# Rotary embedding on one core: all slab loads in SyncE's ring, the tables in ScalarE's ring as 4 KB descriptors

## The chip, the cores and the metric

The kernel runs on one core of a Trainium2 chip. The metric is device time in microseconds (us), lower is better. Three runs of the kernel before gave 163.01, 164.19 and 165.96 us; the median is 164.19. One more execution was profiled.

## The reference

The input `x` is 16 x 512 x 1024 in float32, 33.55 MB; the output has the same size. Each row of 1024 is 16 heads of 64. `cos` and `sin` have one row of 32 numbers for each of the 512 positions (64 KB each), and all batches and heads share them.

```
x = x.reshape(batch, seq, num_heads, head_dim)
x1, x2 = x[..., :half_dim], x[..., half_dim:]
cos = cos[None, :, None, :]
sin = sin[None, :, None, :]
rotated = np.concatenate([
    x1 * cos - x2 * sin,
    x1 * sin + x2 * cos
], axis=-1)
```

## The kernel before, in words

**Tiling.** The batch is cut into 8 slabs (s = 0 to 7) of two batch entries, 4 MB each. A slab is one SBUF tile of 128 partitions x 8192 float32: partition p holds 8 consecutive rows (32 KB, contiguous in DRAM). Six tiles exist (`slots = 6`), so slab 6 reuses the tile of slab 0, and slab 7 that of slab 1, once the earlier slab's store has landed.

**Loads.** `load(s)` (L59 to L63) issues one 4 MB DMA. Slabs 0 to 5 go on SyncE's queue (SP), slabs 6 and 7 on GpSimd's (POOL). On SP the order is: slab 0, `cos`, `sin` (L72), slabs 1 to 5. The loads of slabs 6 and 7 are issued from the end of the main loop (L141), after the stores of slabs 0 and 1.

**Tables.** `cos` and `sin` land as 64 partitions x 256 float32 (8 positions in a partition, 1 KB each, 64 descriptors a table). GpSimd casts them to bf16 (L91). Since partitions p and p + 64 of a slab need the same positions, four matmuls (L96) with selection matrices of 0 and 1 (or -1) `pick` (built by GpSimd, L81 to L87) copy the 64 rows to 128 partitions and lay out `cos|cos` and `sin|-sin` for the 64 columns of a head in PSUM tile `acc`. VectorE copies that to the bf16 tile `tab` (L102). Every multiplication in the main loop reads `tab`.

**Main loop.** Slabs 1 to 5 are one pass each, slabs 0, 6 and 7 two passes of half a slab. A pass is: ScalarE casts float32 to bf16 (L121, into the upper part of the tile's own bytes); VectorE multiplies twice by the tables (L131) and adds with the halves of each head swapped (L134); ScalarE casts back to float32 (L137). After the last pass of a slab ScalarE's queue issues the 4 MB store (L139). A cast in (L121) of a whole slab takes 7.0 us, a cast out (L137) 7.0 us, of half a slab 3.6 us each; VectorE needs 13.3 us for a slab.

**Order of the queues.** The program's framework orders the instructions of each engine. In the trace ScalarE's order is, from slab 2 on: cast in of slab s + 2, store of slab s, cast out of slab s + 1, and so on. So the store of slab s stands behind a cast that waits for the load of slab s + 2. At the end: cast in 6a, store 4, cast out 5, cast in 6b, store 5, cast out 6a, cast in 7a, cast out 6b, cast in 7b, store 6, cast out 7a, cast out 7b, store 7 (a and b are half slabs).

DMA packets of a slab are 32 KB, 8 for each of the core's 16 DMA engines. The profile calls SP's ring q1, ScalarE's ring q10 and GpSimd's q0. The framework has 8 completion counters for the DMAs that SP and ScalarE issue, and takes them in turn. A DMA waits until the earlier user of its counter has landed: the sixth slab load (slab 5) is issued at 13.18 us, when slab 0 has landed.

Of the kernel before, what the change touches and what calls it, by code (L numbers as in the profile page):

```python
# [2 lines left out]

# [4 lines left out]


@with_exitstack  # L10
def kernel(
    ctx: ExitStack,
    tc: tile.TileContext,
    x: bass.AP,
    cos: bass.AP,
    sin: bass.AP,
    num_heads: int,
    out: bass.AP,
):
    nc = tc.nc  # L20
    P = nc.NUM_PARTITIONS

    batch, seq, dim = x.shape
    nh = num_heads
    hd = dim // nh
    half = hd // 2
    bf16 = mybir.dt.bfloat16
    f32 = mybir.dt.float32

    nb = 2  # L30
    slots = 6
    nslabs = batch // nb
    rpp = nb * seq // P
    W = rpp * dim
    SP = seq // rpp
    TW = rpp * half

    out_flat = out.rearrange("b s h d -> b s (h d)")

    singles = ctx.enter_context(tc.tile_pool(name="singles", bufs=1))  # L40
    slabs = ctx.enter_context(tc.tile_pool(name="slabs", bufs=slots))
    psum = ctx.enter_context(tc.tile_pool(
        name="psum", bufs=1, space=bass.MemoryType.PSUM))


    def dram(t, s, a=0, n=W):
        return bass.AP(tensor=t.tensor, offset=t.offset + s * nb * seq * dim + a,
                       ap=[[W, P], [1, n]])


    def view(t, offset, *dims):
        return dataclasses.replace(t, offset=t.offset + offset,
                                   ap=[t.ap[0], *[list(d) for d in dims]])


    slab = {}


    def load(s):  # L59

        queue = nc.sync if s < slots else nc.gpsimd
        slab[s] = slabs.tile([P, W], f32, tag="slab", name="slab")
        queue.dma_start(out=slab[s], in_=dram(x, s))  # L63


    load(0)


    cos_sb = singles.tile([SP, TW], f32, tag="cos_sb")
    sin_sb = singles.tile([SP, TW], f32, tag="sin_sb")  # L70
    for t, src in ((cos_sb, cos), (sin_sb, sin)):
        nc.sync.dma_start(out=t, in_=bass.AP(  # L72
            tensor=src.tensor, offset=src.offset, ap=[[TW, SP], [1, TW]]))

    for s in range(1, slots):
        load(s)

    pick = singles.tile([SP, 2 * P], bf16, tag="pick")  # L80
    nc.gpsimd.memset(pick, 0.0)  # L81
    for g in range(2):
        part = view(pick, g * P, (SP, P // SP), (1, SP))
        nc.gpsimd.affine_select(  # L84
            out=part, in_=part, compare_op=mybir.AluOpType.not_equal,
            fill=1.0 - 2.0 * g, base=0, pattern=[[0, P // SP], [-1, SP]],
            channel_multiplier=1)  # L87

    tab1 = singles.tile([SP, 2 * TW], bf16, tag="tab1")
    for i, t in enumerate((cos_sb, sin_sb)):  # L90
        nc.gpsimd.tensor_copy(out=view(tab1, i * TW, (1, TW)), in_=t)  # L91

    acc = psum.tile([P, 2 * rpp * hd], f32, tag="acc")
    for i in range(2):
        for h in range(2):
            nc.tensor.matmul(  # L96
                view(acc, i * rpp * hd + h * half, (hd, rpp), (1, half)),
                view(pick, i * h * P, (1, P)),
                view(tab1, i * TW, (half, rpp), (1, half)),
                start=True, stop=True)  # L100
    tab = singles.tile([P, 2 * rpp * hd], bf16, tag="tab")
    nc.vector.tensor_copy(out=tab, in_=acc)  # L102

    passes = []
    for s in range(nslabs):
        n = rpp if 1 <= s < nslabs - 2 else rpp // 2
        passes += [(s, r, n) for r in range(0, rpp, n)]  # L110


    def halves(u):
        s, r, n = u
        t = slab[s].bitcast(bf16)
        return [view(t, (2 * r + i * n) * dim, (1, n * dim)) for i in range(2)]


    def cast(u):
        s, r, n = u  # L120
        nc.scalar.copy(out=halves(u)[0], in_=view(slab[s], r * dim, (1, n * dim)))  # L121


    cast(passes[0])
    for i, u in enumerate(passes):
        s, r, n = u
        if i + 1 < len(passes):
            cast(passes[i + 1])
        lo, up = halves(u)
        for t, a in ((up, 0), (lo, rpp * hd)):  # L130
            nc.vector.tensor_mul(  # L131
                out=t, in0=lo,
                in1=view(tab, a + r * hd, (hd, n), (0, nh), (1, hd)))
        nc.vector.tensor_add(  # L134
            out=up, in0=up, in1=view(lo, half, (hd, n * nh), (-half, 2), (1, half)))

        nc.scalar.copy(out=view(slab[s], r * dim, (1, n * dim)), in_=up)  # L137
        if r + n == rpp:
            nc.scalar.dma_start(out=dram(out_flat, s), in_=slab[s])  # L139
            if s + slots < nslabs:  # L140
                load(s + slots)  # L141


# [1 line left out]
_INS = ['x', 'cos', 'sin', 'num_heads']  # L145
_OUTS = [((16, 512, 16, 64), 'float32')]

_NUMBERS = {'num_heads': 16}


# [26 lines left out]
```

## Time and profile before

The profiled execution took 163.56 us, 0.63 us under the median of the three runs. Its span, from the first to the last instruction that the profile shows, is 161.8 us, so 1.8 us lie around the span. Times below are us from the span's start.

| slab | load issued | load landed | store issued | store landed |
|---|---|---|---|---|
| 0 | 0.74 | 13.16 | 37.48 | 61.13 |
| 1 | 2.37 | 23.39 | 51.31 | 87.83 |
| 2 | 3.00 | 33.10 | 65.16 | 108.41 |
| 3 | 3.49 | 45.46 | 93.97 | 120.59 |
| 4 | 4.02 | 64.82 | 107.93 | 130.26 |
| 5 | 13.18 | 93.94 | 121.45 | 139.96 |
| 6 | 61.77 | 95.16 | 135.62 | 149.62 |
| 7 | 88.40 | 114.53 | 149.80 | 160.90 |

`cos` and `sin` were issued at 1.17 and 1.74 and had landed at 13.52 and 13.86. "Landed" is the last of the 16 completion records of a DMA, one from each DMA engine. A store "issued" at 37.48 is the moment at which ScalarE's queue hands it to the DMA rings. Read a row from left to right for one slab's way through the kernel, and the columns "landed" together for what the DMA engines did: 16 slabs of 4 MB went through them.

| engine | busy, us | share of the span |
|---|---|---|
| DVE (VectorE) | 108.5 | 67% |
| ACT (ScalarE) | 113.2 | 70% |
| POOL (GpSimd) | 3.0 | 2% |
| PE (TensorE) | 1.0 | 1% |

### The profile page before, as it was taken

The page shows a single profiled execution, that of the slowest core. Times are in us where ns is not written, and L with a number is a line of the kernel's source. Part 1 is how long each engine was busy: PE and PEld are TensorE (multiplying, and loading weights), DVE is VectorE, ACT ScalarE, POOL GpSimd, SP SyncE. Part 2 cuts the span into 40 slices and gives each one's busy share as a digit, 9 for nine tenths or more (in the row PEclk, how much of TensorE's full clock was granted, in tenths as well). Part 3 has the DMA queues.
Part 4 walks back from the last instruction along what each step waited for, and adds up shares of the span by engine and source line. Part 5 has one row for each costly group of instructions (what it writes and reads, how often), then busy time and mean ns, then how long its engine had stood idle before and what let it go on. Part 6 is the DMA issues. An engine that isn't in the chain of part 4 may idle for free.

```text
span 161.8 us, 157 instructions
## 1 busy us (share of the span) xinstructions
PE 1.0 (1%) x4; PEld 0.5 (0%) x4; DVE 108.5 (67%) x34; ACT 113.2 (70%) x23; POOL 3.0 (2%) x11
## 2 busy tenths in 40 slices
PE   0002000000000000000000000000000000000000
PEld 0000000000000000000000000000000000000000
DVE  0002899999899989989991000999991999991000
ACT  3007929999999999999500079995799999928000
POOL 2001000000000001000001000000000000000000
DMA  7999999999999999999899999999999999996996
GB/s 243 405 389 421 462 446 389 454 454 389 405 470 421 405 470 421 413 454 429 389 478 429 389 486 421 397 478 421 405 470 421 421 462 413 429 454 284 389 389 259
DMA packets 2464, 67.24 MB, mean 416 GB/s; under 512 B 288, under 2 KB 416, under 8 KB 416
## 3 DMA queue, kind: packets, MB, share of 16 engines
q10 hardware_dynamic: 1152, 33.55, 48.1%
q1 hardware_dynamic: 1024, 25.30, 37.1%
q0 software_dynamic: 288, 8.39, 12.1%
HBM read 33.69 MB, written 33.55 MB: 416 GB/s over the span
## 4 chain that ended last, share of the span: by engine, by line
ACT 34%; issue 23%; DMA 13%; DVE 12%; another core or an unknown queue 9%; SPq 1%; ACTq 0%
ACT slab L137 23%; DMA slab<-in_x_dram 13%; ACT slab L121 11%; DVE slab L131 8%; DVE slab L134 4%; SPq L72 1%; SPq L63 0%; ACTq L137 0%; ACTq L121 0%
## 5 line engine op out<-in xcount | busy, mean ns | idle before, releaser
L131 DVE TENSOR_TENSOR slab<-slab,tab 128x4096 bf16<-128x4096 bf16 (+1 forms) x22 | 71.7, 3261 | 22.2 <-ACT slab L121 21.7
L121 ACT CAST slab<-slab 128x4096 bf16<-128x4096 f32 (+1 forms) x11 | 56.6, 5153 | 29.3 <-DMA slab<-in_x_dram 29.3
L137 ACT CAST slab<-slab 128x4096 f32<-128x4096 bf16 (+1 forms) x11 | 56.6, 5154 | 6.6 <-DVE slab L134 6.5
L134 DVE TENSOR_TENSOR slab<-slab 128x4096 bf16<-128x4096 bf16 (+1 forms) x11 | 35.9, 3261 | 0.3
L102 DVE CAST tab<-acc 128x1024 bf16<-128x1024 f32 x1 | 1.2, 1224 | 15.1 <-PE acc L96 15.1
L63 POOL DMA_DIRECT2D slab<-in_x_dram x2 | 1.2, 611 | 73.4 <-DMA out_dram<-slab 73.4
L121 ACT ACT_TABLE_LOAD x1 | 1.3, 1283 | 0.7 <-PEq L158 0.7
L96 PE MATMUL acc<-tab,pick 64*128 64x256 bf16 x4 | 1.0, 403 | 14.0 <-POOL tab L91 14.0
L91 POOL CAST tab<-cos_sb 64x256 bf16<-64x256 f32 x1 | 0.4, 389 | 11.9 <-DMA cos_sb<-in_cos_dram 11.9
L84 POOL TENSOR_SCALAR_AFFINE_SELECT pick<-pick 64x128 bf16<-64x128 bf16 x2 | 0.5, 286 | 0.1
L96 PEld LDWEIGHTS <-pick 64*128 64x128 bf16 x4 | 0.5, 121 | 14.1 <-issue 12.5
L91 POOL CAST tab<-sin_sb 64x256 bf16<-64x256 f32 x1 | 0.4, 393 | 0.0
L81 POOL MEMSET pick<- 64x256 bf16 x1 | 0.3, 304 | 0.3 <-POOLq L158 0.3
L158 POOL MEMSET const-float32-0.0<- 128x1 f32 x1 | 0.1, 103 | 0.2 <-issue 0.2
L158 POOL MEMSET const-bfloat16-1.0<- 128x1 bf16 x1 | 0.1, 106 | 0.0
L158 POOL MEMSET const-uint8-127<- 128x1 uint8 x1 | 0.1, 106 | 0.0
L158 POOL MEMSET const-float32-1.0<- 128x1 f32 x1 | 0.1, 103 | 0.0
## 6 DMA issues: line engine op xcount, KB each, us to landing
out_dram<-slab ACTq DMA_DIRECT2D x8, 4096.0 KB, 23.0
slab<-in_x_dram SPq DMA_DIRECT2D x6, 4096.0 KB, 36.0
slab<-in_x_dram POOLq DMA_DIRECT2D x2, 4096.0 KB, 29.8
cos_sb<-in_cos_dram SPq DMA_DIRECT2D x1, 64.0 KB, 12.3
sin_sb<-in_sin_dram SPq DMA_DIRECT2D x1, 64.0 KB, 12.1
```

Of the source, the lines that this page charges most:

```text
L63: queue.dma_start(out=slab[s], in_=dram(x, s))
L72: nc.sync.dma_start(out=t, in_=bass.AP(tensor=src.tensor, offset=src.offset, ap=[[TW, SP], [1, TW]]))
L81: nc.gpsimd.memset(pick, 0.0)
L84: nc.gpsimd.affine_select(out=part, in_=part, compare_op=mybir.AluOpType.not_equal, fill=1.0 - 2.0 * g, base=0, pattern=[[0, P // SP], [-1 ...
L91: nc.gpsimd.tensor_copy(out=view(tab1, i * TW, (1, TW)), in_=t)
L96: nc.tensor.matmul(view(acc, i * rpp * hd + h * half, (hd, rpp), (1, half)), view(pick, i * h * P, (1, P)), view(tab1, i * TW, (half, rpp) ...
L102: nc.vector.tensor_copy(out=tab, in_=acc)
L121: nc.scalar.copy(out=halves(u)[0], in_=view(slab[s], r * dim, (1, n * dim)))
L131: nc.vector.tensor_mul(out=t, in0=lo, in1=view(tab, a + r * hd, (hd, n), (0, nh), (1, hd)))
L134: nc.vector.tensor_add(out=up, in0=up, in1=view(lo, half, (hd, n * nh), (-half, 2), (1, half)))
L137: nc.scalar.copy(out=view(slab[s], r * dim, (1, n * dim)), in_=up)
L158: nc = _bacc.Bacc("TRN2", target_bir_lowering=False, num_devices=1)
```

## The change

All eight slab loads are issued on SP's queue; the loads of slabs 6 and 7 still come from the same place in the loop and wait for the stores of slabs 0 and 1. The two tables leave SP's queue for ScalarE's, where they are issued at the start. Each table is now 16 descriptors of 4 KB: 32 positions to a partition, on every eighth partition of a tile `raw` of 128 x 1024 float32 (`cos` on partitions 0, 8, 16, ..., `sin` on 4, 12, 20, ...). VectorE clears `raw` first. GpSimd casts all of `raw` to bf16 in one instruction, and builds 12 selection matrices in place of 2 (one memset of 128 x 1536 and 12 selects). Each of the four parts of `acc` is now the sum of four matmuls, one for each group of 8 positions in a partition, so 16 matmuls in place of 4. `tab` holds the same numbers in the same places, and the main loop is unchanged.

```diff
     def load(s):
-
-        queue = nc.sync if s < slots else nc.gpsimd
         slab[s] = slabs.tile([P, W], f32, tag="slab", name="slab")
-        queue.dma_start(out=slab[s], in_=dram(x, s))
+        nc.sync.dma_start(out=slab[s], in_=dram(x, s))
...
+    TR = 16
+    TQ = seq // TR // rpp
+    TC = seq * half // TR
+    raw = singles.tile([P, TC], f32, tag="raw")
+    nc.vector.memset(raw, 0.0)
+    def load_tables(queue):
+        for i, src in enumerate((cos, sin)):
+            to = dataclasses.replace(
+                raw, offset=raw.offset + 4 * i * raw.ap[0][0],
+                ap=[[P // TR * raw.ap[0][0], TR], [1, TC]])
+            queue.dma_start(out=to, in_=bass.AP(
+                tensor=src.tensor, offset=src.offset, ap=[[TC, TR], [1, TC]]))
     load(0)
-    cos_sb = singles.tile([SP, TW], f32, tag="cos_sb")
-    sin_sb = singles.tile([SP, TW], f32, tag="sin_sb")
-    for t, src in ((cos_sb, cos), (sin_sb, sin)):
-        nc.sync.dma_start(out=t, in_=bass.AP(
-            tensor=src.tensor, offset=src.offset, ap=[[TW, SP], [1, TW]]))
+    load_tables(nc.scalar)
     for s in range(1, slots):
         load(s)
-    pick = singles.tile([SP, 2 * P], bf16, tag="pick")
+    pick = singles.tile([P, 3 * TQ * P], bf16, tag="pick")
     nc.gpsimd.memset(pick, 0.0)
-    for g in range(2):
-        part = view(pick, g * P, (SP, P // SP), (1, SP))
-        nc.gpsimd.affine_select(
-            out=part, in_=part, compare_op=mybir.AluOpType.not_equal,
-            fill=1.0 - 2.0 * g, base=0, pattern=[[0, P // SP], [-1, SP]],
-            channel_multiplier=1)
+    for g in range(3):
+        for j in range(TQ):
+            part = view(pick, (g * TQ + j) * P + j, (SP, P // SP), (TQ, TR))
+            nc.gpsimd.affine_select(
+                out=part, in_=part, compare_op=mybir.AluOpType.not_equal,
+                fill=-1.0 if g == 2 else 1.0, base=-4 if g else 0,
+                pattern=[[0, P // SP], [-(P // TR), TR]], channel_multiplier=1)
-    tab1 = singles.tile([SP, 2 * TW], bf16, tag="tab1")
-    for i, t in enumerate((cos_sb, sin_sb)):
-        nc.gpsimd.tensor_copy(out=view(tab1, i * TW, (1, TW)), in_=t)
+    raw_b = singles.tile([P, TC], bf16, tag="raw_b")
+    nc.gpsimd.tensor_copy(out=raw_b, in_=raw)
     acc = psum.tile([P, 2 * rpp * hd], f32, tag="acc")
-    for i in range(2):
-        for h in range(2):
+    for g, at in ((0, 0), (0, half), (1, rpp * hd), (2, rpp * hd + half)):
+        for j in range(TQ):
             nc.tensor.matmul(
-                view(acc, i * rpp * hd + h * half, (hd, rpp), (1, half)),
-                view(pick, i * h * P, (1, P)),
-                view(tab1, i * TW, (half, rpp), (1, half)),
-                start=True, stop=True)
+                view(acc, at, (hd, rpp), (1, half)),
+                view(pick, (g * TQ + j) * P, (1, P)),
+                view(raw_b, j * TW, (half, rpp), (1, half)),
+                start=j == 0, stop=j == TQ - 1)
```

## The prediction

> **What bounds the kernel now.** I read the page from the top: busy shares, slices, queues. No compute engine passes 70%, but the DMA row is at 9 in all but a few slices, and the queues add up.
>
> ```profile
> span 161.8 us, 157 instructions
> ...
> DMA  7999999999999999999899999999999999996996
> ...
> q10 hardware_dynamic: 1152, 33.55, 48.1%
> q1 hardware_dynamic: 1024, 25.30, 37.1%
> q0 software_dynamic: 288, 8.39, 12.1%
> ```
>
> The three shares make 97.3%, 157.4 of 161.8 us: the 16 DMA engines work nearly all the time. By windows they moved 429 GB/s with one ring (13.2 to 37.5 us), 424 with two (41.5 to 61.5) and 437 with three (66 to 90): how the work is spread over rings hardly changes the rate. What can be gained are the three places where they stand still: slice 0 (start), the 6 in slice 36, the 6 in the last. I open the end with the DMA view for 140 to 161.8 us (40 slices of 0.55 us).
>
> ```profile
> DMA  9999590959699890000909109090909169090000
> GB/s 481 481 421 541 240 721 0 721 240 661 301 421 541 361 601 0 0 0 0 962 0 902 60 0 962 0 962 0 962 0 902 60 301 661 0 962 0 0 0 0
> ```
>
> Slices 15 to 18 (148.2 to 150.4 us) move nothing. Single empty slices mean nothing (packets are counted where they start, and last 1.2 us); four in a row are a hole. Why it is there, the timeline says:
>
> ```profile
> 146.16 3.60 ACT L137 CAST slab<-slab 128x4096 f32<-128x4096 bf16 x1 [3.56 <-DVE slab L134]
> 149.80 0.34 ACTq L139 DMA_DIRECT2D out_dram<-slab  x1
> ```
>
> Store 7 is issued at 149.80, after the last cast out, while store 6 had landed at 149.62: the rings were empty. Back to back, stores land 9.68 us apart (130.26, 139.96, 149.62). Store 7 lands 11.28 after store 6, so the hole costs 1.60 us. Then I asked why ScalarE was late with its last cast. The waits show it:
>
> ```profile
> ACT slab L121 <- DMA slab<-in_x_dram: 29.3, 3, 15.0
> ...
> DVE tab L102 <- PE acc L96: 15.1, 1, 15.1
> PE acc L96 <- POOL tab L91: 14.0, 1, 14.0
> ...
> POOL tab L91 <- DMA cos_sb<-in_cos_dram: 11.9, 1, 11.9
> ```
>
> The lower three are the table chain at the start, over by 16.3 us. The 15.0 us is the cast of slab 5, from 78.97 to 93.97: slab 5 lands at 93.94. Its load was in SP's ring long before; it crept, because from 66 us on three rings share the engines, as the DMA view for 68 to 84 us shows:
>
> ```profile
> q0 software_dynamic: 72, 2.36, 34.7%
> q1 hardware_dynamic: 70, 2.29, 33.3%
> q10 hardware_dynamic: 70, 2.29, 33.2%
> ```
>
> A third each. Slab 6 (q0), needed later, took a third of the bandwidth from slab 5 (q1), needed next, and landed 1.2 us after it.
>
> **The change part by part.**
>
> *Slabs 6 and 7 behind slab 5 on SP.* Nothing changes up to 61.1 us (store 0 lands, slab 6 is issued). From then on there are two rings; rows for two rings are at hand: store 0 and load 4 ran side by side from 41.8 to 61.13, so a slab takes 19.4 us of a half share. Store 1: 61.1 + 19.4 = 80.5 (now 87.8). Slab 5, after slab 4 at 64.8: 84.2 (now 93.9). Slab 6: 103.6 (now 95.2). Slab 7, whose load is issued when store 1 lands at 80.5 and so waits in the ring: 123.0 (now 114.5). Stores 2 and 3: 99.9 and 119.3. Issue costs 0.33 to 0.58 us of SP's time a load, and behind them SP has only the end's waits; on POOL nothing stood behind them either. So these cost 0; the cover is the load before it in the ring, and if that ran dry, a new start costs 1.4 us (store 7: 11.1 from issue to landing, less 9.7).
>
> *ScalarE with these landings,* in the order it has now, 7.0 and 3.6 us a cast: cast 5 and store 3 at 84.2; cast out 4 91.2 to 98.2; cast 6a waits for slab 6 at 103.6, with it store 4; cast out 5 to 114.2, cast 6b, store 5 at 114.3; cast out 6a to 121.3; cast 7a waits for slab 7, 123.0 to 126.6; cast out 6b 130.2, cast 7b, store 6 at 130.3. From the start of cast 7a to the end of the last cast out it is now 128.33 to 149.76, 21.4 us: store 7 at 123.0 + 21.4 = 144.4. Every store is issued before the one ahead of it has landed (store 4 103.6 before 119.3, store 5 114.3 before about 130, store 6 130.3 before 140, store 7 144.4 before 149.6). The 29.3 us of waits move, they don't vanish, but the hole closes. After 13 slabs' worth (130.26 now) three stores remain: 130.26 + 3 x 9.68 = 159.30 against 160.90. Gain 1.6; bounds 0 (hole comes back whole) and 1.6 (there is no more in it).
>
> *Tables in DMA time.* Slab 0 to slab 1 is 10.23 us between landings, slab 1 to slab 2 9.71: the tables cost 0.52 now. Later, 128 KB at the 434 GB/s of whole slabs (4.19 MB in 9.7 us) are 0.3. Bounds 0.3 and 0.52 (no better than now): I take a gain of 0.2, the slab rate being nearest to 4 KB pieces on 16 engines, though the bytes are few.
>
> [...]
>
> *Tables in time for VectorE.* `tab` is ready at 16.28 now and first read at 16.82, when ScalarE's first cast ends. After: the memset of `raw`, 128x1024, bounded by the copy L102 of that size, 1.22 us, from 0.74 to 2.0; two issues on ScalarE's queue at 0.34 to 0.58, to 3.2 (ScalarE is idle until slab 0 is there, so nothing queues behind them but the 1.28 us table load). Start in a ring beside a full one: store 0 was issued at 37.48 and had first packets at 41 to 41.8, so up to 4.3; to an empty one 1.4. Two rounds of packets of 1.2 us: landed between 6 and 10. GpSimd: memset of 6 times the elements of the 0.30 one, 1.8; 12 selects at 0.29, 3.4: done at 6.0, before the tables at the late end. Cast of 4 times the elements of 0.39: 1.6. 16 matmuls at 0.25 (four took 1.01): 4.0, at most 0.41 each, 6.6. Copy 1.2. So `tab` at 13 to 17, at worst 19.4. First use is at 16.8, and 0.2 later with slab 0's landing. A delay up to 3.4 us is still hidden: the second half slab's add ends at 30.4 and ScalarE, busy with slab 1, takes it at 33.84. Beyond that it would eat into ScalarE's idle time before cast 5. So 0, and at the worst 0.
>
> **Sum.** 163.56 - 1.6 - 0.2 = 161.8 against the profiled execution. The median of the three runs is 0.63 higher; one execution and three runs cannot say which is typical, so I add half of it: **162.1 us**, 1.3% under 164.19.
>
> **The rivals.**
>
> *A: the hole stays.* The gap closes only if slab 7 lands by 126.8: store 7 must be issued 1.4 us before 149.6, and needs 21.4 from the landing. My 123.0 leaves 3.8. For it: cast 7a waits for slab 7 now, which it did not before (landed 114.5, cast at 128.3), so slab 7's lateness goes into the end. Against it: half shares were steady from 44 to 61 us. With a landing at 128.3, store 7 is at 149.8 again: 163.4 to 164.2, no change.
>
> *B, slower: a load held up by a completion counter.* The waits of SP's queue have a load that waited for another load, though its tile was free:
>
> ```profile
> SPq L63 <- DMA slab<-in_x_dram: 8.7, 1, 8.7
> ```
>
> The counters are taken in turn by 8, and the change puts 18 DMAs on them in place of 16. Eight places back is a DMA that landed long ago in every order I can think of; but if slab 7's load had to wait for store 3 (119.3) instead of store 1, the ring would be dry from 103.6. It would start at 120.7 beside store 4, land 19.4 later near 140, and store 7 would go at 161.5 and land 11.1 later, at 172.6: 175 us. It decides where slab 7 lands after 128.3, and makes over 2% from 131.6 (3.3 us more). The same holds if the engines' new order puts a cast that waits for slab 7 ahead of older casts out.
>
> *C: faster than the hole.* Nothing to gain is left but the start (1.9 us idle until the first packet) and the end; 160.9 or less needs the runs to fall low, as 163.01 did under 164.19.
>
> *D: the change does nothing:* the tables are off the path already (0.54 us of slack at 16.82), and the bytes are the same. If slab 5's early landing is no use because the end is decided elsewhere, this is A.
>
> **How the numbers follow.** Forecast 0.64, A 0.20, B 0.12, C 0.04. The likeliest one's own range is 160.8 to 163.4: 162.1 less the 1.2 us that the lowest run lay under the median, and up to the sum with no gain from the tables and the whole 0.63, and 0.7 of run-to-run difference. The range reaches through A, whose runs may lie as high as its 164.2 and 0.9 more: 160.8 to 165.1; beyond lies B. The bounds are 160.9 and 167.5, 2% either way, about what a measurement of this kernel can tell from no change. Faster: C and the low edge of the forecast, 0.11. Slower: B and little else, 0.13. Same: 0.76.
>
> **What would show it.** Right: no q0 at all; slab 5 cast near 84, slab 6 near 104, slab 7 near 123; no run of empty slices near 149; store 7 issued before store 6 lands, its issue to landing well over 11.1 us; ScalarE's 15.0 us wait broken into some 5 us each before slabs 5 and 6; L102 ending before 17.5. Wrong: a cast of slab 7 after 127, a wait of SP for anything but store 0, store 1 and slab 0, or ScalarE's order changed. A `tab` after 20 us would mean that the tables starve beside a full ring.

## The result and the profile after

The changed kernel takes 162.09 us (median of 6 runs, 161.88 to 162.21), the kernel before 163.81 in the same comparison (163.01 to 166.01). The ratio is 0.9912, with a 95% interval of 0.9883 to 0.994: a gain of 0.9%, small but outside the noise. The profiled execution took 161.88 us, its span is 160.1. Some executions of the kernel before, e1, e8 and e9 are 2 to 13 us longer, and those over 1.5% above the kernel's fastest are left out of the ratios; in the two that were profiled (e1 and e9) two of the 16 DMA engines finish slabs up to 15 us after the others, the reason is not known, and none of the 44 runs with the tables in ScalarE's ring was left out.

The page of the changed kernel, the same lines as before:

```profile
span 160.1 us, 200 instructions
...
DMA  7999999999999999999999999999999999999994
...
q1 hardware_dynamic: 1152, 33.55, 49.3%
q10 hardware_dynamic: 1216, 33.69, 48.8%
```

q0 is gone, and so is the 6 in slice 36: from slice 1 to 38 every digit is 9. The shares make 98.1% of 160.1, 157.1 us, the work of before (157.4); what went is idle time. Where three rings had a third of the engines each, the DMA view of 68 to 84 us now shows two halves:

```profile
q1 hardware_dynamic: 121, 3.44, 49.8%
q10 hardware_dynamic: 119, 3.38, 48.9%
```

The DMA view of 138.4 to 160.1 us, the last 21.7:

```profile
DMA  0909092992909092962909091948909090920000
GB/s 0 967 0 966 0 846 121 483 483 121 846 0 966 0 846 121 664 302 121 846 0 966 0 906 60 785 181 362 604 0 966 0 966 0 846 121 0 0 0 0
```

Up to the last packets there are never two empty slices in a row; in the kernel before there were four (148.2 to 150.4 us). The timeline of ScalarE shows the middle of it, from slab 5 on (start, duration, instruction, and in brackets the idle time ahead of it):

```profile
84.17 7.02 ACT L129 CAST slab<-slab 128x8192 bf16<-128x8192 f32 x1 [3.85 <-DMA slab<-in_x_dram]
...
103.53 3.60 ACT L129 CAST slab<-slab 128x4096 bf16<-128x4096 f32 x1 [5.42 <-DMA slab<-in_x_dram]
...
122.95 3.60 ACT L129 CAST slab<-slab 128x4096 bf16<-128x4096 f32 x1 [1.88 <-DMA slab<-in_x_dram]
...
140.63 3.60 ACT L145 CAST slab<-slab 128x4096 f32<-128x4096 bf16 x1 [3.46 <-DVE slab L142]
144.27 0.34 ACTq L147 DMA_DIRECT2D out_dram<-slab  x1
```

The one wait of 15.0 us has become three, for slabs 5, 6 and 7: 3.85, 5.42 and 1.88 us, 11.2 in all. The landings and stores against the forecast:

| | before | forecast | after |
|---|---|---|---|
| slab 5 landed | 93.94 | 84.2 | 84.15 |
| slab 6 landed | 95.16 | 103.6 | 103.51 |
| slab 7 landed | 114.53 | 123.0 | 122.87 |
| store 1 landed | 87.83 | 80.5 | 80.42 |
| last store issued | 149.80 | 144.4 | 144.27 |
| store 6 landed | 149.62 | 149.6 | 149.44 |
| last store landed | 160.90 | 159.3 | 159.09 |
| `tab` ready | 16.28 | 13 to 17, at worst 19.4 | 18.70 |

The last store is handed over 5.2 us before store 6 has landed, and lands 9.65 us after it, back to back, not 11.28.

### The profile page after: what moved, and what is told of

It reads as the page before. It is cut to its first block, busy times and chain, and to the rows that moved or that the text cites. A ratio compares the mean times of both kernels' runs of the same rounds, so it can differ in the third digit from the quotient of the medians.

```text
span 160.1 us, 200 instructions
## 1 busy us (share of the span) xinstructions
PE 3.6 (2%) x16; PEld 2.3 (1%) x16; DVE 109.3 (68%) x35; ACT 113.3 (71%) x23; POOL 4.7 (3%) x18
## 4 chain that ended last, share of the span: by engine, by line
DMA 50%; DVE 21%; ACT 8%; issue 7%; PE 2%; POOLq 1%; ACTq 0%; DVEq 0%; SPq 0%
DMA slab<-in_x_dram 26%; DMA out_dram<-slab 17%; DVE slab L139 14%; DMA raw<-in_sin_dram 6%; DVE slab L142 6%; ACT slab L145 5%; ACT slab L129 3%; PE acc L104 2%; DVE tab L110 1%; POOLq L180 1%; DVE raw L69 1%; ACTq L77 0%; POOLq L99 0%; DVEq L139 0%; SPq L61 0%
## 5 line engine op out<-in xcount | busy, mean ns | idle before, releaser
L129 ACT CAST slab<-slab 128x4096 bf16<-128x4096 f32 (+1 forms) x11 | 56.6, 5153 | 23.1 <-DMA slab<-in_x_dram 23.1
L104 PE MATMUL acc<-raw_b,pick 128*128 128x256 bf16 x16 | 3.6, 415 | 13.9 <-POOL raw_b L99 13.9
L104 PEld LDWEIGHTS <-pick 128*128 128x128 bf16 x16 | 2.3, 142 | 14.7 <-issue 11.3
L93 POOL TENSOR_SCALAR_AFFINE_SELECT pick<-pick 128x32 bf16<-128x32 bf16 x12 | 2.1, 257 | 0.1
L69 DVE MEMSET raw<- 128x1024 f32 x1 | 0.9, 912 | 1.0 <-PEq L166 1.0
L89 POOL MEMSET pick<- 128x1536 bf16 x1 | 1.4, 1377 | 0.3 <-POOLq L166 0.3
L99 POOL CAST raw_b<-raw 128x1024 bf16<-128x1024 f32 x1 | 1.0, 1036 | 8.5 <-DMA raw<-in_sin_dram 8.5
```

Of the source, the lines that this page charges most:

```text
L69: nc.vector.memset(raw, 0.0)
L93: nc.gpsimd.affine_select(out=part, in_=part, compare_op=mybir.AluOpType.not_equal, fill=-1.0 if g == 2 else 1.0, base=-4 if g else 0, pat ...
L99: nc.gpsimd.tensor_copy(out=raw_b, in_=raw)
L104: nc.tensor.matmul(view(acc, at, (hd, rpp), (1, half)), view(pick, (g * TQ + j) * P, (1, P)), view(raw_b, j * TW, (half, rpp), (1, half)), ...
```

## The experiments

**Theory and rivals.** Theory O (order): the gain is the hole ahead of the last store. It closes because slab 5 no longer shares the engines with slab 6 from a third ring, and it needs nothing of the tables' new path. Rival T: the tables make the gain. Rival R: it is GpSimd's ring that is slow. A second pair is about the end: *threshold* (slab 7 may be late until 126.8 at no cost, and from there each us costs one) against *every-us* (its lateness always shows) and *bytes alone* (it never does).

**e1_loads_only**: one line of the kernel before.

```diff
-        queue = nc.sync if s < slots else nc.gpsimd
+        queue = nc.sync
```

> The kernel before, with one edit: all eight slab loads on SyncE's queue; the tables stay as they were. Theory O (order): what closed the hole ahead of the last store is that slab 5 no longer shares with slab 6 from a third ring. Then slab 5 lands near 84, slab 7 near 123, the last store is issued near 144.4, before store 6 has landed, and the time is 161.9 to 162.2 us, the whole of the change's gain. Slab 2 lands at 33.1, as before, against 33.27 in the changed kernel, if the tables in ScalarE's ring cost those 0.17. Theory T (tables): the new table path makes the gain; this kernel takes 163.4 to 164 and the last store is issued at about 149.8.

161.96 us, ratio 0.9849 (0.979 to 0.9907). The whole gain is there with the old tables. The profile that came with it is of an execution of 172.91 us, and only its first 35 us are used below; **e8_loads_only_again** ran the same kernel beside the changed one.

> The kernel before with all slab loads on SyncE's queue, once more, for an undisturbed profile and beside the changed kernel on the same chip. Theory O: slab 2 lands at 33.1, slab 5 near 84, slab 7 near 122.8, the last store is issued near 144.2; 161.9 to 162.0 us, 0.1 to 0.2 under the changed kernel, whose tables cost 0.17 more DMA time.

162.08 us, ratio 0.9907 (0.9886 to 0.9927). The two lines from its timeline:

```profile
84.30 7.02 ACT L121 CAST slab<-slab 128x8192 bf16<-128x8192 f32 x1 [5.08 <-DMA slab<-in_x_dram]
...
144.41 0.34 ACTq L139 DMA_DIRECT2D out_dram<-slab  x1
```

Slab 5 landed at 84.28, slab 7 at 123.01, store 6 at 149.63, and the last store, issued 5.2 us ahead of that, at 159.29: no hole. Slab 2, expected at 33.1, landed at 33.35, later than in the changed kernel's profile (33.27). The 0.17 us that I put on the new table path is within what profiles differ by.

**e10_changed_again**: the changed kernel on the same chip.

> The changed kernel itself, on the same chip as the two others: 162.0 to 162.2 us, runs within 0.4 us of each other, slab 2 at 33.27.

162.00 us (161.85 to 162.43), ratio 0.9905 (0.9886 to 0.9924). Slab 2 landed at 33.74 here, not 33.27, and the runs differ by 0.6 us, not 0.4. With and without the tables' new path the time is the same to 0.1 us. Slab 5 landed at 83.30, 0.85 earlier than in the first profile of this kernel, and the last store landed 0.53 later (159.62): with the hole closed the end no longer follows slab 5.

**e2_tables_only**: the other half of the change alone.

```diff
-        nc.sync.dma_start(out=slab[s], in_=dram(x, s))
+        queue = nc.sync if s < slots else nc.gpsimd
+        queue.dma_start(out=slab[s], in_=dram(x, s))
```

> The changed kernel, with the loads of slabs 6 and 7 back on GpSimd's queue: the tables' part of the change alone. Theory O: the three rings share again from 66 us, slab 5 lands near 94, the last store is issued after store 6 has landed, the hole of about 1.6 is back, 163.5 to 163.8 us, and runs differ by a us or more as they did before. Theory T: 162.1 us, no hole.

163.69 us (162.36 to 164.12), ratio 0.9989 (0.9962 to 1.0017): no gain. T has fallen. The profiled execution was the quickest of the twelve, 162.36, and its timeline is worth a look beside that of before:

```profile
92.76 7.02 ACT L130 CAST slab<-slab 128x8192 bf16<-128x8192 f32 x1 [12.99 <-DMA slab<-in_x_dram]
...
148.60 0.34 ACTq L148 DMA_DIRECT2D out_dram<-slab  x1
```

Slab 5 landed at 92.74, 1.20 earlier than in the profile of before; the last store was issued at 148.60, 1.20 earlier; the execution took 1.20 us less (162.36 and 163.56). The distance from slab 5's landing to the last store is 55.86 us in both. In these two executions with three rings the end follows slab 5, us for us. I had expected the last store after store 6's landing (149.62); it was issued 1.0 us ahead of store 6's landing, and landed 10.07 after it; 0.4 of the hole was left in this execution. Slab 5's lead was there as soon as slab 3 had landed (44.16 against 45.46); where it comes from the runs do not say. The other executions of e2, most of them 1 us and more longer, were not profiled.

**e3_stores_pool**: two rings, one of them GpSimd's.

```diff
-            nc.scalar.dma_start(out=dram(out_flat, s), in_=slab[s])
+            nc.gpsimd.dma_start(out=dram(out_flat, s), in_=slab[s])
```

> The changed kernel, with the eight stores issued on GpSimd's queue in place of ScalarE's: two rings again, loads in order, but one of the two is GpSimd's. ScalarE's order differs in one place (both halves of slab 6 are cast in before slab 5 is cast out), which by hand puts the last store at about 148. Theory O: it is the number of rings that share with slab 5, not whose ring; slab 5 lands near 84, slab 7 near 123, 162.1 to 162.8 us. Theory R (ring): packets of GpSimd's ring are slower, as in the three-ring stretch, where they took 1.24 to 1.27 us against 1.213; 64 packets an engine then cost 2 to 4 us more: 164 to 166.

162.51 us (162.24 to 162.72), ratio 0.9882 (0.9814 to 0.995). The queues of its page:

```profile
q1 hardware_dynamic: 1152, 33.55, 49.3%
q0 software_dynamic: 1152, 33.55, 48.4%
q10 hardware_dynamic: 64, 0.13, 0.2%
```

All stores went through q0; their packets took 1.213 us, slab 5 landed at 82.95, slab 7 at 121.64, and the last store was issued at 146.81 (148 by hand). R has fallen: the same ring that took a third of slab 5's bandwidth is harmless as one of two, when it carries the stores. (In the view of 68 to 84 us of the kernel before, 34.7% for 72 packets is 1.23 us a packet, a little under the 1.24 to 1.27 that R started from.) No run keeps three busy rings with the loads in order, so the number of rings and the order of the loads are not told apart. The 0.4 us over the changed kernel lie behind the last landing (159.07 of a span of 160.5), outside this question.

**e5, e6, e7: how late may slab 7 be?** Three kernels that move the issue of slab 7's load and leave ScalarE's order as it is. In e5 and e6 slab 7 gets the tile of slab 2 or 3, so its load waits for that slab's store.

```diff
-        slab[s] = slabs.tile([P, W], f32, tag="slab", name="slab")
+        at = {6: 0, 7: 2}.get(s, s)
+        slab[s] = slabs.tile([P, W], f32, tag=f"slab{at}", name="slab")
...
-            if s + slots < nslabs:
-                load(s + slots)
+            if s in (0, 2):
+                load(6 if s == 0 else 7)
```

(3 in place of 2 in e6; the pool then has one buffer to a tag.) In e7 the load waits for slab 6 to land:

```diff
+        if s == 7:
+            nc.gpsimd.tensor_copy(out=view(slab[7], 0, (1, 1)), in_=view(slab[6], 0, (1, 1)))
         nc.sync.dma_start(out=slab[s], in_=dram(x, s))
```

> The changed kernel, with slab 7 in the tile of slab 2 in place of slab 1, so that its load waits for store 2 (landed 99.8) and not store 1 (80.4). ScalarE's order is the same. Theory threshold: nothing moves until SyncE's ring runs dry at 103.5; issued at 99.8, the load's first packets follow slab 6 within 1 us or less; slab 7 lands by 124, the last store is issued by 145.4, before store 6 has landed: 162.0 to 162.5 us. Theory every-us: slab 7's way is the critical chain, and an issue 19 us later shows in the end: over 163.

> The same with slab 7 in the tile of slab 3, so that its load waits for store 3. SyncE's ring is dry from 103.5; the stores then have the engines alone and store 3 lands near 111.4, not 119.1. The load's first packets come 1.4 to 4.3 us later (112.8 to 115.7), at half share it lands 19.4 later (132.2 to 135.1), the last store is issued 21.4 later (153.6 to 156.5), lands 11.1 after that, and 2.7 us lie behind: 167.3 to 170.3 us. Theory threshold needs that. If the end is set by bytes alone, 162.1 to 163.

> The changed kernel, with slab 7's load held until slab 6 has landed (GpSimd copies one column of slab 6 into slab 7's tile first; the load overwrites it). The ring is dry from 103.5 to the load's first packets, 1.4 to 4.3 us after an issue at about 104: 105.4 to 108.3. The stores run alone meanwhile, and slab 7 lands 19.4 later, 124.8 to 127.7. Theory threshold (harmless up to a landing at 126.8, since the last store then is issued 1.4 us before store 6 lands): 162.0 to 163.0 us, with the last store issued at 146.2 to 149.1. Theory every-us: 2 to 5 us over 162.1.

The kernel before took 163.70 to 167.16 us in that comparison, which makes its ratios wide (0.9822, 1.0292 and 0.9889, with intervals some 0.02 wide), so I set the three beside the changed kernel's 162.09 (from another comparison; e5, at 161.98, suggests that the two agree):

| kernel | slab 7 issued | landed | last store issued | last store landed | profiled, us | median, us |
|---|---|---|---|---|---|---|
| changed | 80.47 | 122.87 | 144.27 | 159.09 | 161.88 | 162.09 |
| e5 | 99.78 | 122.80 | 144.19 | 159.09 | 161.88 | 161.98 |
| e7 | 104.93 | 128.04 | 149.44 | 160.54 | 163.31 | 163.15 |
| e6 | 110.86 | 133.79 | 155.19 | 166.28 | 169.07 | 169.76 |

An issue 19 us later (e5) costs nothing: the load only waited in the ring, and slab 7 landed no later. In e7 the ring ran dry and slab 7 landed 5.2 us later than in the changed kernel (and 0.3 later than I had expected at the latest), 1.2 past 126.8; the time rose by 1.1 (profiled 1.4). In e6 it came 7.0 past it, and the profiled time is 7.2 over the changed kernel's. From the landing to the last store's issue it is 21.4 us each time. From e7 to e6 slab 7 lands 5.75 us later and the profiled time grows by 5.76; followed back at that rate, the cost reaches 0 at a landing of 126.6. Threshold holds; every-us falls with e7, where some 4 of the 5.2 us cost nothing, bytes alone with e6. No run has slab 7 land between 123.0 and 126.8. The two lines that carry e6:

```profile
133.87 3.60 ACT L130 CAST slab<-slab 128x4096 bf16<-128x4096 f32 x1 [12.87 <-DMA slab<-in_x_dram]
...
155.19 0.34 ACTq L148 DMA_DIRECT2D out_dram<-slab  x1
```

and its DMA view of 140 to 167.3 us, with the hole back and wider: seven empty slices in a row, of 0.68 us each, from 150.9 to 155.7 (the first two still carry packets, which are counted where they start):

```profile
GB/s 0 0 768 0 768 0 768 0 768 528 240 768 0 768 0 768 0 0 0 0 0 0 0 768 0 768 0 768 480 288 768 0 768 0 768 96 672 0 0 0
```

**e4_tables_64_act**: all loads on SyncE's queue, the old tables of 64 descriptors on ScalarE's.

```diff
-        queue = nc.sync if s < slots else nc.gpsimd
+        queue = nc.sync
...
-        nc.sync.dma_start(out=t, in_=bass.AP(
+        nc.scalar.dma_start(out=t, in_=bass.AP(
```

> The kernel before with all loads on SyncE's queue and its tables (64 descriptors of 1 KB each) on ScalarE's queue: what the 16 descriptors of 4 KB are for. In the changed kernel cos landed at 8 to 10 and sin at 10.8 to 12.6 us. Theory turn: beside a full ring each descriptor, a completion too, waits for one 32 KB packet of the other ring, 1.21 us. Here an engine has 4 + 1 descriptors a table, so cos lands near 12, sin near 18, the tables are ready near 21, VectorE starts near 21 in place of 18.8, and the end does not notice: 162.0 to 162.4. Theory burst: a ring's turn takes many descriptors; sin lands by 13 as in the changed kernel, VectorE starts by 17.

162.14 us, ratio 0.9857 (0.979 to 0.9925). The start of its timeline, then that of the changed kernel:

```profile
12.49 0.39 POOL L91 CAST tab<-cos_sb 64x256 bf16<-64x256 f32 x1 [10.86 <-DMA cos_sb<-in_cos_dram]
...
17.96 0.39 POOL L91 CAST tab<-sin_sb 64x256 bf16<-64x256 f32 x1 [5.08 <-DMA sin_sb<-in_sin_dram]
...
20.35 6.82 DVE L131 TENSOR_TENSOR slab<-slab,tab 128x4096 bf16<-128x4096 bf16 x3
```

```profile
12.77 1.04 POOL L99 CAST raw_b<-raw 128x1024 bf16<-128x1024 f32 x1 [8.52 <-DMA raw<-in_sin_dram]
...
18.79 6.82 DVE L139 TENSOR_TENSOR slab<-slab,tab 128x4096 bf16<-128x4096 bf16 x3
```

`sin` landed at 17.91, 5.47 us after `cos` at 12.44: five entries for an engine, four pieces and a completion. In the changed kernel there are two, and 2.65 us between the tables (9.97 and 12.62). That is about one 32 KB packet of the other ring, 1.21 us, for each entry. The packets of e4 show it piece by piece: in each of the windows 5.9 to 6.9, 7.1 to 8.2, 8.4 to 9.5 and 9.8 to 10.9 us ScalarE's ring starts 16 pieces of `cos`, as many as there are engines, and SyncE's ring 16 packets of 32 KB; the 16 completions follow between 11.1 and 12.2. Burst has fallen. So fewer descriptors do bring the tables earlier in ScalarE's ring, by 5.3 us though they were issued 1.2 us later; the end does not notice it.

**e9_tables16_sync**: the new layout in the old ring, behind slab 0.

```diff
-    load_tables(nc.scalar)
+    load_tables(nc.sync)
```

> The changed kernel with its tables (16 descriptors of 4 KB each) issued on SyncE's queue behind slab 0, as the tables were before. It parts the layout from the ring. [...] 161.8 to 162.1 us.

Its six runs took 162.61 to 175.28 us, so its time says nothing. The first 35 us of its profile are like the others': slab 0 landed at 13.25, slab 1 at 23.40, slab 2 at 33.11. Less the 9.71 of a slab, the tables took 0.44 us there. With the old layout it was 0.52 in the kernel before, 0.63 in e8 and 0.39 in e1 (slab 0 at 13.67, slab 1 at 23.77). One profile of the new layout lies inside what three of the old one differ by: no difference between the layouts is shown, and the 0.3 us that I had taken can't be ruled out from it.

## Why the prediction was right, point by point

- **The bound and the hole**: right. DMA time hardly moved (157.4 to 157.1 us), and the hole of 1.60 us went; the profiled executions differ by 1.68. Against all runs that go into the ratio it is 0.9%, not the forecast's 1.3%: the 164.19 that it was set against was the median of three runs, one of them 165.96. e1 and e8 show that the loads' order alone does it, e2 that the rest of the change does not.
- **The half-share ledger**: right to 0.2 us in every row of the table above but that of `tab`. It rested on one row, store 0 beside load 4 at 19.4 us.
- **ScalarE's order**: unchanged, and the 21.4 us from slab 7's landing to the last store held in e4 to e8 and e10 too. That the 29.3 us of waits for loads would only move was not so: 23.1 are left. It changed nothing in the sum.
- **Tables in DMA time, 0.2 gained**: not borne out as a term. e10 and e8, with and without the new path, differ by 0.08 us, less than the runs of either, and e9 shows 0.44 where I had taken 0.3, inside the 0.39 to 0.63 of the old layout; 0 would have been the better value.
  The sum comes out all the same, since 163.56 - 1.6 = 161.96 is as near to 161.88 as 161.8 is: that is luck.
- **Tables in time**: the conclusion (0 at the end) was right, the middle was wrong, and the sign "L102 ending before 17.5" did not come. I let `sin` land by 10 at the latest; it landed at 12.62. I had counted two rounds of packets, and not that a completion takes a turn as well as a piece; and the first pieces started 4.1 to 5.8 us after their issue, not up to 4.3. GpSimd's and TensorE's parts were shorter than I had them (1.04 and 3.6 us), which put `tab` at 18.70. VectorE started 2.0 us later than before, and the second half slab's add ended at 32.3, still 1.7 ahead of ScalarE's turn at 34.0. But the 3.4 us of slack were read at slab 0 alone. One slab later ScalarE did wait for VectorE: its cast out of slab 1 began at 45.62 after 1.11 us of waiting, where it had begun at 44.27 without a wait, and stores 1 and 2 were issued 1.4 us later than before (52.67 and 66.51). What hid that is the ring: store 1 stands in it behind store 0, which landed at 61.08.
- **The half of 0.63 added for the median**: the changed kernel's profiled run lay 0.21 under its median. That is a guess that came out well, no more.
- **Rival C** (160.9 or less) was not seen, the lowest run of the changed kernel is 161.85, and **D** (no change) is outside the interval. **Rival A** was priced rightly: its threshold of 126.8 is within 0.2 us of what e7 and e6 give. **Rival B**'s mechanism was not seen. In the traces its counters are eight semaphores: in the kernel before they are raised by 16 DMAs, two each, and the load of slab 5 waits 8.7 us for the one that slab 0's load raised; in the changed kernel 18 DMAs raise them, and slab 7's load takes the one that slab 1's had raised, landed at 23.54, so it was free long before the issue at 80.47. Its price was too high. With SyncE's ring dry the stores run alone: in e6 store 3 landed at 110.81, not 119.3, slab 7 at 133.79, not 140, and the time was 169.1, not 175. The load's start beside the stores' ring was dearer than I had it: its first packets came at 114.9, 4.1 us after the issue, not 1.4.

No version tried is clearly faster: e1, e4, e5, e8 and e10 lie within 0.13 us of the changed kernel. What is left idle is 1.7 us ahead of the first packet and 1.0 behind the last.

## What to carry to other kernels

When the DMA engines are busy nearly all the time, look for the slices in which they are not, and ask which transfer had to come earlier to fill them. Here a third ring added no bandwidth (429, 424 and 437 GB/s with one, two and three), it took a third of the engines (34.7%) and left the load that was needed next 33.3% in place of a half (49.8%); loads that are needed in order did better in one ring (e8: 162.08 us, ratio 0.9907). Work out by how much the last load may be late before the last store is, and what happens when its ring runs dry.

## What the runs showed that I had not expected

Beside a ring full of 32 KB packets, each entry of another ring waited for about one such packet (1.21 us), the entry that reports completion too: 2.65 us for two entries in the changed kernel, 5.47 for five in e4. A load queued behind others in its ring could be issued 19 us later without any effect (e5: landed at 122.80, against 122.87), while one whose ring had run dry paid for a start beside the full ring of the stores: in e7 slab 7 was issued 1.4 us after slab 6's landing in the changed kernel, its first packets came 3.7 us after its issue (108.67), and it landed 5.2 us later than there. And e2's runs differ more, 162.36 to 164.12 us against 161.85 to 162.43 for the twelve of the changed kernel; that its end hangs on slab 5's share is seen in one profile of it and one of the kernel before, and that this is why its runs differ is not shown.
